# A hybrid encoder layer on one core: inputs laid out by the host, and the input stage written out in order on three engines

## The chip, the cores and the metric

The kernel runs on one core of a Trainium2 chip. The metric is the device time of one launch in microseconds: 2149.15 us is the median of three runs of the kernel before (2146.5 to 2149.57).

Five engines of the core work side by side, each through its own queue of instructions: TensorE (PE in the profile, its weight loads PEld), VectorE (DVE), ScalarE (ACT), GpSimd (POOL) and SyncE (SP), which here issues nearly all transfers. They wait for each other through semaphores. An instruction that waits holds up everything behind it in its engine's queue.

## The reference

The layer has a token-mixing and a channel-mixing half. Only the first steps matter for the change:

```python
mod = (c_act @ w_ada[l] + b_ada[l])[:, None, :]
shift_t, scale_t, gate_t, shift_f, scale_f, gate_f = jnp.split(mod, 6, axis=-1)
h = x * (1.0 + scale_t) + shift_t
proj = h @ w_in[l]
qkv_a, z_a, beta_raw, a_raw, q_b, k_b, v_b, gates = jnp.split(proj, IN_SPLITS, axis=-1)
```

`c_act` is silu of a vector of 1024, `w_ada` is 1024 x 6144, `x` is 1024 tokens x 1024 features, `w_in` 1024 x 9232. From `proj` the layer forms a gated DeltaNet (8 heads, a delta rule in chunks of 64 tokens) and an attention over the own chunk and the 8 before it (16 heads), merges both by sigmoid gates, projects, adds and normalises; then an up projection to 2 x 2816, a causal convolution of width 3, a gated product, a down projection and a second normalisation. All is float32.

## The kernel before, in words

**Data.** `h` is kept with features on the 128 partitions, in 8 chunks of 128 features (`hh`, `hl`: 128 x 8 x 1024). Every float32 operand of a large product is split into a high part (rounded to the format that TensorE takes at full pace) and a low part, the rest; a product is then three: high x high, high x low, low x high. A dense block is 128 output columns: 2 halves of 512 tokens x 8 chunks x 3 products = 48 products of shape 128x512.

**The input stage** (lines 346 to 453) makes `h` and its first uses. For each chunk j of 128 features it

- loads the 1024 x 128 columns of `w_ada` for shift and for scale (`wa`, 1 MB) and 128 columns of `x` (`xj`, 512 KB);
- sums `w_ada` times `csil` = silu(c) over the 8 row blocks on DVE (`acc`, L371 and L373: one scalar product, then seven fused multiply-adds). The first two chunks are summed alone (256 columns an instruction), the other six in pairs (512 columns);
- adds over the partitions with two fp32 products against a column of ones (`pmods`, L407), which TensorE runs as two instructions each;
- adds the bias on ACT (L410), transposes the eight 128 x 128 blocks of `x` on PE (`px`, L416), and applies scale and shift on ACT twice per half of 512 tokens, once in float32 (`h32`, L417) and once rounded (`hh`, L418); DVE takes the difference (`hl`, L419).

While the chunks arrive, three blocks of `w_in` are already multiplied chunk by chunk (`dense_chunk`, `pfirst`, products of L290): the first head's keys and queries and the first gate block, "k", "g" and "q". Chunk j's products are traced two chunks behind its modulation (`LAG0 = 2`). 3 x 48 = 144 products result. After them come 32 products for the beta and decay columns (`pabt`, L447), eight small transposes (`pab`), and the per-feature vectors, each loaded as rows and transposed on PE (`vectors`, `pv`, L323).

**What sets the order.** A planner that simulates the engines and transfers places each instruction in its engine's queue. `tc.issue_after(ins)` puts what is traced in its block behind `ins` on the same engine; in the input stage it is used only to keep the DVE sums one behind the other and a few late loads behind the last `x`. Further on, from the first head on, PE's order is written out by hand (`lane.pinned`): waves of the delta rule between the dense products of the next head.

**Transfers.** All weights are read from the reference's arrays. A block of 128 columns is 1024 runs of 512 bytes (`kview`); `w_up` likewise; the rows of `w_ada` for the gates are 2 KB, those of `w_down` and `w_o` 4 KB. `load_split` loads into a ring of three buffers (`raw`), ACT makes the high part (L188), POOL or DVE the low part (L191).

`class Chain` (L162) wraps an engine: each instruction issued through it stands behind the one before. Before the change it is used only in the later stages.

Of the kernel before, what the change touches and what calls it, by code (L numbers as in the profile page):

```python
# [17 lines left out]
P = 128  # L18
S = 1024
D = 1024  # L20
NK = 8
# [26 lines left out]
HEAD0 = 8  # L48
FILL = (120, 124, 100, 112, 125, 130, 140, 110)
# [12 lines left out]
def _at(group, step_, n, first=0):  # L62
# [8 lines left out]
    "acc0": _at("G", 256, 2, 2048), "acc1": _at("G", 512, 2), "v0": _at("G", 128, 4, 2816), "rab": _at("G", 0, 1, 3328), "abt": _at("G", 0, 1, 1024),  # L71
# [69 lines left out]
def hybrid_layer(  # L141
# [40 lines left out]
    def load_split(h, l, src, he, le, a=1, cuts=1):  # L182

        raw = W.tile([P, 1024], F32, tag="raw", bufs=RB, name=nm("raw"))
        SP.dma_start(raw.rearrange("p (a b) -> p a b", a=a) if a > 1 else raw, src)
        if cuts == 1:
            return split(h, l, raw, he, le)
        he.copy(h, raw)  # L188
        for i in range(cuts):
            N = slice(1024 // cuts * i, 1024 // cuts * (i + 1))  # L190
            le.tensor_tensor(l[:, N], raw[:, N], f(h[:, N]), ALU.subtract)  # L191

    def kview(w, c0, n):
        return w[:, c0:c0 + n].rearrange("(k p) n -> p k n", p=P)

    x2, out2 = x[0], out[0]
    w_ada2, w_in2 = w_ada[0], w_in[0]
# [116 lines left out]
    def vectors(o, group, eng=SP):  # L314

        v = ring("v0", [P, P])
        r = 0
        for s_ in group:
            n = s_.shape[0]
            eng.dma_start(v[r:r + n, :], s_)  # L320
            r += n
        pv = pbank(nm("pv"), "px")
        PE.transpose(pv[:, :r], v[:r, :], ident[:r, :r])  # L323
        ACT.copy(vt[:, o:o + r], pv[:, :r])

    def rows(v):
        return v.rearrange("(r p) -> r p", p=P)
# [4 lines left out]
    GC = 7 * D + 2 * HA  # L332
# [3 lines left out]
    vectors(VO["c"], [c.rearrange("o (r p) -> (o r) p", p=P), rows(b_ada[0])], ACT)  # L336
# [12 lines left out]
    def ab_weights():  # L349
        raw = ring("rab", [P, NK, 16])  # L350
        SP.dma_start(raw, kview(w_in2, 4 * D, 16))
        wab = ring("wab", [P, NK, 32], F32R)
        split(wab[:, :, 0:16], wab[:, :, 16:32], raw, DVE, DVE)
# [4 lines left out]
        ACT.activation(al, al, AF.Exp)  # L358
        return wab, al, dtb

    def ada_cols(j, n):
        kk = NK // 2 // n
        wa = [ring("wa", [P, kk, 2, n * P]) for _ in range(2 * n)]
        for i in range(2 * n):
            for m in range(2):
                SP.dma_start(wa[i][:, :, m, :],
                             w_ada2[kk * P * i:kk * P * i + kk * P, m * D + j * P:m * D + j * P + n * P].rearrange(
                                 "(k p) n -> p k n", p=P))
        acc = ring(f"acc{n - 1}", [P, 2, n * P])
        with tc.issue_after(mark0["acc"]) if mark0 else nullcontext():  # L370
            DVE.tensor_scalar(acc, wa[0][:, 0], csil[:, 0:1], None, ALU.mult)  # L371
            for k in range(1, NK):
                i = DVE.scalar_tensor_tensor(acc, wa[k // kk][:, k % kk], csil[:, k:k + 1], acc,  # L373
                                             ALU.mult, ALU.add)
        mark0["acc"] = i.ins
        for q in range(n):
            accs[j + q] = acc[:, :, q * P:q * P + P]
            xs.append(load_x(j + q))

    def load_x(j):  # L380
        xj = ring("xj", [P, NT, P])
        mark0["x"] = SP.dma_start(xj, x2[:, j * P:j * P + P].rearrange("(t p) n -> p t n", p=P)).ins
        return xj

    LEAD, LAG = 2, LAG0

    first = {"k": (D, "d", "d"), "g": (GC, "m", "m"), "q": (0, "d", "i")}
    wfirst, pend = {}, {}

    def first_weights(m):  # L390
        wfirst[m] = wblock(kview(w_in2, first[m][0], P), NK, ACT, DVE)

    def dense_chunk(k):
        for m in first:
            if m not in pend:
                pend[m] = [pbank(nm("pfirst"), r) for r in first[m][1:]]
            for n in range(2):
                mark0["mm"] = mm_fm(pend[m][n], wfirst[m], hhk, hlk, n, [k]).ins

    xs = []  # L400
    for j in range(LEAD):
        ada_cols(j, 1)
        first_weights("kg"[j])
    for j in range(NK):
        pm = pmods[:, 2 * j:2 * j + 2]
        for m in range(2):
            PE.matmul(pm[:, m:m + 1], accs[j][:, m, :], ones[:, 0:1], start=True, stop=True)  # L407
        cs = ring("mc", [P, 2])
        for m in range(2):
            ACT.activation(cs[:, m:m + 1], pm[:, m:m + 1], AF.Identity, bias=bb[:, j, m:m + 1])  # L410
        h32 = ring("h32", [P, S])
        for n in range(2):
            N = slice(512 * n, 512 * n + 512)
            px = pbank(nm("px"), "px")
            for t in range(4):
                tr = PE.transpose(px[:, t * P:t * P + P], xs[j][:, 4 * n + t, :], ident)  # L416
            ACT.activation(h32[:, N], px, AF.Identity, bias=cs[:, 0:1], scale=cs[:, 1:2])  # L417
            ACT.activation(hh[:, j, N], px, AF.Identity, bias=cs[:, 0:1], scale=cs[:, 1:2])  # L418
# [1480 lines left out]
```

## Time and profile before

The profile shows one execution. Its busy times by engine are shares of the span, the time from the first to the last instruction.

| | us |
|---|---|
| median of three runs | 2149.15 |
| the profiled execution, whole | 2149.37 |
| its span | 2147.7 |
| PE busy | 2101.4 |
| DVE busy | 1428.9 |
| ACT busy | 988.3 |
| POOL busy | 430.8 |
| queue 1, transfers: share of 16 engines | 39.3% |

A line of the profile names a line of the kernel, an engine, an operation and tiles as out<-in, with the shape in partitions x elements. Products are pipelined: one takes about 0.4 us, but the next one starts 0.23 us after it. The view of the stretches gives busy time per engine between two moments; the chain of waits follows what released each instruction, back from the end.

### The profile page before, as it was taken

To read this page: it belongs to the slowest core of one execution; us is meant where nothing else is said; L and a number is where in the kernel's file an instruction comes from. 1 tells how busy PE (TensorE), PEld (TensorE's weight loads), DVE (VectorE), ACT (ScalarE), POOL (GpSimd) and SP (SyncE) were. 2 spreads that over 40 slices of the span, in tenths; PEclk is the share of its full clock that TensorE was granted. 3 is DMA by queue.
4 is the path that set the end of the run, shared out by engine and by line. 5 is a ranking of instruction groups with operands and counts; after the bars stand their busy time and mean duration, and the time that the engine had idled before them with its cause. 6 is when DMAs were issued, how large, how long until landed. Compare 5 with 4: busy or idle time off the path is not lost.

```text
span 2147.7 us, 31798 instructions
## 1 busy us (share of the span) xinstructions
PE 2101.4 (98%) x11577; PEld 1762.4 (82%) x11577; DVE 1428.9 (67%) x3008; ACT 988.3 (46%) x2159; POOL 430.8 (20%) x391
## 2 busy tenths in 40 slices
PE   7999999999999999999999999999999999999998
PEld 5787788888887888989897888888788888888886
DVE  6478576776777754556556534358987788875744
ACT  4544453454544434565555532236554444452431
POOL 0233233233332322110211224200210000000000
PEclk9999999999999999999999999999999999999999
DMA  9232324333233244544547443422332222285440
GB/s 298 68 104 82 123 77 121 99 91 118 72 116 124 63 143 144 158 130 110 161 124 228 140 134 117 142 89 79 98 96 66 85 89 89 98 283 183 162 157 40
DMA packets 243167, 263.04 MB, mean 122 GB/s; under 512 B 23034, under 2 KB 189491, under 8 KB 243011
## 3 DMA queue, kind: packets, MB, share of 16 engines
q1 hardware_dynamic: 242931, 260.99, 39.3%
q8 instruction: 91, 1.49, 0.3%
q14 instruction: 65, 0.53, 0.1%
q10 hardware_dynamic: 80, 0.03, 0.0%
HBM read 207.89 MB, written 58.83 MB: 124 GB/s over the span
## 4 chain that ended last, share of the span: by engine, by line
PE 84%; DVE 8%; ACT 3%; DMA 2%; issue 2%; SPq 1%; POOL 0%; DVEq 0%; ACTq 0%; POOLq 0%
PE pup L1617 17%; PE pdn L1771 11%; PE pqkv L532 7%; PE pqk L532 6%; PE pgt L532 6%; PE pv L532 5%; PE pwo L1459 4%; PE pbr L290 4%; PE pbr L532 4%; PE po L532 4%; PE pz L532 4%; PE ps L532 3%; PE pp L532 2%; PE pfirst L290 1%; DMA raw<-in_w_in_dram 1%
## 5 line engine op out<-in xcount | busy, mean ns | idle before, releaser
L191 POOL TENSOR_TENSOR wl<-raw,wh 128x512 fp32r<-128x512 f32 x170 | 223.7, 1339 | 529.5 <-ACT wh L188 434.4
L1617 PE MATMUL pup<-hh,wop 128*128 128x512 f32 x704 | 224.2, 390 | 0.4 <-ACT G L1654 0.4
L1617 PE MATMUL pup<-t,wop 128*128 128x512 f32 x792 | 189.4, 392 | 1.3 <-DVE cc L1658 0.8
L1617 PEld LDWEIGHTS pup<-t,wop 128*128 128x128 f32 x792 | 148.6, 188 | 34.7 <-DVE cc L1658 1.2
L1771 PE MATMUL pdn<-dop,dop 128*128 128x512 f32 x696 | 161.6, 391 | 0.0
L1617 PEld LDWEIGHTS pup<-hh,wop 128*128 128x128 f32 x704 | 132.1, 188 | 29.1 <-ACT G L1654 0.8
L1771 PEld LDWEIGHTS pdn<-dop,dop 128*128 128x128 f32 x696 | 130.7, 188 | 28.3
L532 PE MATMUL pqkv<-hh,wl 128*128 128x512 f32 x352 | 141.3, 401 | 0.0
L532 PE MATMUL pqkv<-hh,wh 128*128 128x512 f32 x352 | 140.1, 398 | 0.0
L532 PE MATMUL pqkv<-hl,wh 128*128 128x512 f32 x352 | 139.9, 398 | 0.0
L1617 PE MATMUL pup<-hl,wop 128*128 128x512 f32 x352 | 137.2, 390 | 0.0
L188 ACT CAST wh<-raw 128x1024 fp32r<-128x1024 f32 x88 | 92.1, 1046 | 89.1 <-DMA raw<-in_w_branch_b_dram 13.4
L1659 POOL TENSOR_TENSOR cc<-cc,G 128x512 f32<-128x512 f32 x22 | 44.4, 2018 | 375.6 <-DVE G L1641 352.4
L1237 ACT ACTIVATE G<-G,ST 128x640 f32<-128x640 f32 (+4 forms) x128 | 89.3, 698 | 56.4 <-DVE ST L1233 55.8
L177 ACT CAST wop<-wr 128x512 fp32r<-128x512 f32 x104 | 61.7, 620 | 97.9 <-DVE wr L1599 67.0
L532 PE MATMUL pqk<-hh,wh 128*128 128x512 f32 x256 | 105.6, 413 | 0.0
L532 PE MATMUL pqk<-hl,wh 128*128 128x512 f32 x256 | 104.1, 407 | 0.0
L532 PE MATMUL pqk<-hh,wl 128*128 128x512 f32 x256 | 103.4, 404 | 0.0
L532 PE MATMUL pgt<-hh,wh 128*128 128x512 f32 x240 | 99.2, 413 | 0.0
L757 DVE TENSOR_TENSOR FT<-FT,G 128x16 f32<-128x16 f32 (+30 forms) x248 | 92.1, 371 | 8.9 <-POOL G L658 2.5
L532 PE MATMUL pgt<-hh,wl 128*128 128x512 f32 x240 | 96.2, 401 | 0.0
L1264 DVE TENSOR_TENSOR pl<-pp,ph 128x512 fp32r<-128x512 f32 (+1 forms) x112 | 72.9, 651 | 34.8 <-ACT ph L1263 34.1
(409 smaller groups left out, 5482.6 us busy)
## 6 DMA issues: line engine op xcount, KB each, us to landing
raw<-in_w_in_dram SPq DMA_DIRECT2D x72, 512.0 KB
wr<-in_w_up_dram SPq DMA_DIRECT2D x44, 512.0 KB
dwr<-in_w_down_dram SPq DMA_DIRECT2D x44, 512.0 KB
raw<-in_w_ada_dram SPq DMA_DIRECT2D x32, 512.0 KB
qk_d<-SA SPq DMA_DIRECT2D x80, 128.0 KB
wa<-in_w_ada_dram SPq DMA_DIRECT2D x32, 256.0 KB
gates_d<-GT SPq DMA_DIRECT2D x32, 256.0 KB
g_d<-G SPq DMA_DIRECT2D x15, 512.0 KB
```

What stands on the lines that cost most here:

```text
L177: he.copy(h, src)
L188: he.copy(h, raw)
L191: le.tensor_tensor(l[:, N], raw[:, N], f(h[:, N]), ALU.subtract)
L290: i = PE.matmul(ps, a[:, k, :], r[k][:, 512 * n:512 * n + 512], start=(k == 0 and a is wh and r is rh), stop=(k == NK - 1 and a is wl))
L532: r = getattr(PE, op)(*args, **kw)
L757: DVE.tensor_tensor(pr[:, :, 0:i + 1], ft[:, :, 0:i + 1], fa[:, i:i + 1, 0:i + 1].to_broadcast([P, 8, i + 1]), ALU.mult)
L1237: ACT.activation(sb[:, 0:n], sb[:, 0:n], AF.Exp, bias=mx[:, nb - 1:nb], scale=-1.0, accum_out=total_of(hd, t))
L1264: DVE.tensor_tensor(pl[:, B, :], pp, f(ph[:, B, :]), ALU.subtract).ins)
L1459: PE.matmul(ps[n], a[:, t, k, :], wo[k][b][:, 512 * n:512 * n + 512], start=(k == 0 and a is mh and b == 0), stop=(k == NK - 1 and a is ml))
L1617: i = PE.matmul(ps, a[:, u, k, :], b[v][k], start=(new and k == 0 and u == 0 and v == 0), stop=(k == 3 and u == 1), skip_group_check=not new)
L1659: self.later(7, lambda: POOL.tensor_tensor(o, o, self.t, ADD))
L1771: PE.matmul(ps[n], self.g[:, u, i * P:i * P + P], self.w[v][:, 512 * n:512 * n + 512], start=(first and u == 0 and v == 0), stop=(last and ...
```

## The change

The host puts the inputs into another layout, so that a load takes one run per partition: `w_in`, `w_up` and the branch weights as blocks of 128 x 1024 with 4 KB per partition, `w_ada` in the order of the loads, `x` also transposed, and the small vectors already in columns. The transposes of `x` and of the vectors on PE fall away.

The input stage is traced anew. PE, DVE and ACT each get a `Chain`, so the order in these three queues is that of the code below. `DSUM` names the chunks whose modulation is still summed on DVE (2, 3, 5, 6, each alone, 256 columns an instruction); for the others (0, 1, 4, 7) PE forms the sum directly, 8 fp32 products against a column of `csil` for shift and 8 for scale. `EARLY` = 24 fp32 products of the tile of ones stand first in PE's queue; their result is not used.

```diff
+DSUM = (2, 3, 5, 6)
+EARLY = 24
...
-        load_split(wh, wl, src, he, le, a, cuts)
+        load_split(wh, wl, src, he, le, cuts)
...
+    def vectors(o, v, eng=SP):
+        eng.dma_start(vt[:, o:o + v.shape[1]], v)
...
+    pe, dve, act = Chain(PE, None), Chain(DVE, None), Chain(ACT, None)
...
+    def fetch(j):
+        wa = [ring("wa", [P, 4, 2, P]) for _ in range(2)]
+        for i in range(2):
+            SP.dma_start(wa[i].rearrange("p k m n -> p (k m n)"), w_col[2 * j + i])
+        was.append(wa)
+        xj = ring("xj", [P, S])
+        mark0["x"] = SP.dma_start(xj, xt2[j * P:j * P + P, :]).ins
+        xs.append(xj)
...
+    def split_weights(m):
+        raw, wh, wl = wfirst[m]
+        if m != "k":
+            act.copy(wh, raw)
+        for N in (slice(0, 512), slice(512, 1024)):
+            dve.tensor_tensor(wl[:, N], raw[:, N], f(wh[:, N]), ALU.subtract)
+        wfirst[m] = [t_.rearrange("p (k n) -> p k n", k=NK) for t_ in (wh, wl)]
+
+    def dense(m, k):
+        if m not in pend:
+            pend[m] = [pbank(nm("pfirst"), r) for r in first[m][1:]]
+        wh, wl = wfirst[m]
+        for a, r in ((wh, hh), (wl, hh), (wh, hl)):
             for n in range(2):
...
+                pe.matmul(pend[m][n], a[:, k, :], r[:, k, 512 * n:512 * n + 512],
+                          start=(k == 0 and a is wh and r is hh), stop=(k == NK - 1 and r is hl))
+
+    def modulate(j):
         pm = pmods[:, 2 * j:2 * j + 2]
         for m in range(2):
-            PE.matmul(pm[:, m:m + 1], accs[j][:, m, :], ones[:, 0:1], start=True, stop=True)
+            if j in accs:
+                pe.matmul(pm[:, m:m + 1], accs[j][:, m, :], ones[:, 0:1], start=True, stop=True)
+            else:
+                for k in range(NK):
+                    pe.matmul(pm[:, m:m + 1], was[j][k // 4][:, k % 4, m, :], csil[:, k:k + 1],
+                              start=(k == 0), stop=(k == NK - 1))
+
+    def scaled(j):
         cs = ring("mc", [P, 2])
+        pm = pmods[:, 2 * j:2 * j + 2]
         for m in range(2):
-            ACT.activation(cs[:, m:m + 1], pm[:, m:m + 1], AF.Identity, bias=bb[:, j, m:m + 1])
-        h32 = ring("h32", [P, S])
+            act.activation(cs[:, m:m + 1], pm[:, m:m + 1], AF.Identity, bias=bb[:, j, m:m + 1])
+        h32s.append(ring("h32", [P, S]))
+        for q, o in enumerate((hh[:, j], h32s[j])):
+            if q and j == 0:
+                act.copy(wfirst["k"][1], wfirst["k"][0])
+            for n in range(2):
+                N = slice(512 * n, 512 * n + 512)
+                act.activation(o[:, N], xs[j][:, N], AF.Identity, bias=cs[:, 0:1], scale=cs[:, 1:2])
+
+    def lows(j):
         for n in range(2):
             N = slice(512 * n, 512 * n + 512)
...
+            dve.tensor_tensor(hl[:, j, N], h32s[j][:, N], f(hh[:, j, N]), ALU.subtract)
+
+    def summed(j, ks):
+        if 0 in ks:
+            accs[j] = ring("acc0", [P, 2, P])
+            dve.tensor_scalar(accs[j], was[j][0][:, 0], csil[:, 0:1], None, ALU.mult)
+        for k in ks:
+            if k:
+                dve.scalar_tensor_tensor(accs[j], was[j][k // 4][:, k % 4], csil[:, k:k + 1], accs[j],
+                                         ALU.mult, ALU.add)
+
+    h32s = []
+    fetch(0)
+    first_weights("k")
+    fetch(1)
+    first_weights("g")
+    first_weights("q")
+    fetch(2)
+    fetch(3)
+    LO, HI = range(4), range(4, NK)
+    early = pbank("early", "px")
+    for i in range(EARLY):
+        pe.matmul(early[:, 0:P], ones, ones, start=True, stop=True)
+    modulate(0)
+    scaled(0)
+    lows(0)
+    split_weights("k")
+    dense("k", 0)
+    modulate(1)
+    scaled(1)
+    lows(1)
+    dense("k", 1)
+    split_weights("g")
+    dense("g", 0)
+    dense("g", 1)
+    split_weights("q")
+    dense("q", 0)
+    summed(2, LO)
+    summed(2, HI)
+    modulate(2)
+    scaled(2)
+    dense("q", 1)
+    for j in range(2, NK):
+        if j + 2 < NK:
+            fetch(j + 2)
+        if j == NK - 2:
+            ab = ab_weights()
+        if j + 1 in DSUM:
+            summed(j + 1, LO)
+        lows(j)
+        if j + 1 in DSUM:
+            summed(j + 1, HI)
+        dense("k", j)
+        if j + 1 < NK:
+            modulate(j + 1)
+            scaled(j + 1)
+        dense("g", j)
+        dense("q", j)
+    wab, al, dtb = ab()
+    mark0["mm"] = pe.ins
```

The remaining edits only address the new layout: `wpart(c0)` in place of `kview(w_in2, c0, P)`, whole blocks of `w_row` in `mod_rows`, and `prep`, which builds the arrays on the host.

More of the change, by code (lines that the diff above doesn't have):

```diff
@@ L180, in split, with load_split @@
         return le.tensor_tensor(l, src, f(h), ALU.subtract).ins
-    def load_split(h, l, src, he, le, a=1, cuts=1):
+    def load_split(h, l, src, he, le, cuts=1):
         raw = W.tile([P, 1024], F32, tag="raw", bufs=RB, name=nm("raw"))
-        SP.dma_start(raw.rearrange("p (a b) -> p a b", a=a) if a > 1 else raw, src)
+        SP.dma_start(raw, src)
         if cuts == 1:
@@ L331, in hybrid_layer @@
     eg = ring("eg", [P, HA, NT])
-    GC = 7 * D + 2 * HA
+    GC = 7 * D
     one = ring("one", [P, 1])
     ACT.activation(one, ones[:, 0:1], AF.Exp)
-    vectors(VO["c"], [c.rearrange("o (r p) -> (o r) p", p=P), rows(b_ada[0])], ACT)
+    vectors(VO["c"], c, ACT)
+    vectors(VO["b_ada"], b_col, ACT)
     ACT.activation(csil, vt[:, 0:8], AF.Exp, scale=-1.0)
@@ L350, in ab_weights @@
         raw = ring("rab", [P, NK, 16])
-        SP.dma_start(raw, kview(w_in2, 4 * D, 16))
-        wab = ring("wab", [P, NK, 32], F32R)
-        split(wab[:, :, 0:16], wab[:, :, 16:32], raw, DVE, DVE)
+        SP.dma_start(raw, w_ab)
         al = ring("al", [P, HA])
@@ L357, in ab_weights @@
         SP.dma_start(dtb, dt_bias.partition_broadcast(P).rearrange("p o h -> p (o h)"))
[L358 to L378, printed above, removed]
@@ L400, in hybrid_layer, with ready @@
[L400 to L404, printed above, removed]
+        def ready():
+            wab = ring("wab", [P, NK, 32], F32R)
+            dve.tensor_copy(wab[:, :, 0:16], raw)
+            dve.tensor_tensor(wab[:, :, 16:32], raw, f(wab[:, :, 0:16]), ALU.subtract)
+            act.activation(al, al, AF.Exp)
+            return wab, al, dtb
+        return ready
+    pe, dve, act = Chain(PE, None), Chain(DVE, None), Chain(ACT, None)
@@ new lines, in hybrid_layer @@
+    first = {"k": (D, "d", "d"), "g": (GC, "m", "m"), "q": (0, "d", "i")}
+    wfirst, pend, was, xs = {}, {}, [], []
+    def fetch(j):
[6 more added lines that the diff above has]
+        xs.append(xj)
+    def first_weights(m):
+        raw = W.tile([P, 1024], F32, tag="raw", bufs=RB, name=nm("raw"))
+        SP.dma_start(raw, wpart(first[m][0]))
+        wfirst[m] = [raw] + [W.tile([P, 1024], F32R, tag=t, bufs=WB, name=nm(t)) for t in ("wh", "wl")]
@@ L412, in hybrid_layer @@
+    def lows(j):
         for n in range(2):
             N = slice(512 * n, 512 * n + 512)
[L414 to L418, printed above, removed]
-            DVE.tensor_tensor(hl[:, j, N], h32[:, N], f(hh[:, j, N]), ALU.subtract)
@@ L420, in hybrid_layer @@
-        if j % 2 == 0 and j + LEAD < NK:
-            ada_cols(j + LEAD, 2)
-        if j == 0:
-            first_weights("q")
-        if j == NK - 1:
-            with tc.issue_after(mark0["x"]):
-                wab, al, dtb = ab_weights()
-        if j >= LAG:
-            with tc.issue_after(tr.ins) if PTR else nullcontext():
-                dense_chunk(j - LAG)
-    for k in range(NK - LAG, NK):
-        dense_chunk(k)
+            dve.tensor_tensor(hl[:, j, N], h32s[j][:, N], f(hh[:, j, N]), ALU.subtract)
@@ L439, in hybrid_layer @@
-        vectors(VO["conv_f"] + 88, [rows(conv_ffn[0, 2])])
+        vectors(VO["conv_a"], conv_a)
+        vectors(VO["norm"], norm_a)
+        vectors(VO["ln1g"], g1_col)
+        vectors(VO["ln1b"], b1_col)
+        vectors(VO["conv_f"], conv_ffn)
     abt = ring("abt", [P, S])[0:32, :]
@@ L547, in halves @@
     def halves(name, col0, use, ready=None):
-        w = None if ready else wblock(kview(w_in2, col0, P), NK)
+        w = None if ready else wblock(wpart(col0), NK)
         for n in range(2):
```

114 lines of the change are left out of this document (62 added, 52 removed).

## The prediction

> **What bounds the kernel now.** I read the page's busy shares first, then the busy time of each engine by stretches of the first 74 us, because every moved instruction lies there.
>
> ```profile
> span 2147.7 us, 31798 instructions
> ...
> PE 2101.4 (98%) x11577; PEld 1762.4 (82%) x11577; DVE 1428.9 (67%) x3008; ACT 988.3 (46%) x2159; POOL 430.8 (20%) x391
> ```
> ```profile
> 8.70:21.50 12.80, 9.77 (x31) 7.75 (x32) 10.46 (x21) 7.16 (x12) 0.00 (x0) 1.00 1.08 345
> 21.50:28.50 7.00, 5.31 (x26) 3.34 (x24) 4.69 (x7) 2.50 (x4) 0.00 (x0) 1.00 1.08 336
> 28.50:64.50 36.00, 35.48 (x185) 29.01 (x186) 20.90 (x33) 20.67 (x39) 0.95 (x1) 1.00 0.67 203
> 64.50:74.10 9.60, 8.61 (x41) 4.24 (x40) 5.25 (x11) 6.53 (x12) 8.88 (x8) 1.00 0.63 176
> ```
>
> TensorE (PE) is busy 98% of the span, so a microsecond won or lost on its queue in the input stage moves the end by about as much. The stretches hold, in order, the busy time of PE, its weight loads, VectorE (DVE), ScalarE (ACT) and GpSimd, then the granted clock, the DMA share and GB/s. Up to 28.5 us the transfers are saturated (share 1.08) and PE has holes. From 28.5 to 64.5 us PE is full: 35.48 of 36.00. I take 64.5 as the end of the first dense products (pfirst, 144 of them) and 74.1 as the first product of the next projection (pqkv).
>
> The same stretches for the pfirst line alone:
>
> ```profile
> 8.70:21.50 12.80, 5.89 (x11) 3.71 (x12) 1.00 1.08 345
> 21.50:28.50 7.00, 4.13 (x14) 1.95 (x12) 1.00 1.08 336
> 28.50:64.50 36.00, 31.81 (x120) 21.27 (x120) 1.00 0.67 203
> ```
>
> Some 24 of the 144 are done by 28.5 us, the other 120 afterwards without a hole. So the change must either have done more by 28.5 us, or be no less dense after it.
>
> **Prices.** From the timeline (start, duration, engine, line; a last x4 is four instructions drawn together):
>
> ```profile
> 0.90 0.17 DVE L219 MEMSET ones<- 128x128 f32 x1 [0.90 <-PEq L1885]
> ...
> 5.89 0.35 DVE L371 TENSOR_SCALAR G<-wa,csil 128x256 f32<-128x256 f32 x1
> 6.28 3.61 DVE L373 SCALAR_TENSOR_TENSOR G<-wa,csil,G 128x256 f32<-128x256 f32 x7
> ...
> 9.94 1.02 PE L407 MATMUL pmods<-ones,G 128*128 128x1 f32 x4
> ...
> 10.52 1.05 ACT L188 CAST wh<-raw 128x1024 fp32r<-128x1024 f32 x1 [5.31 <-DMA raw<-in_w_in_dram]
> ...
> 11.47 0.41 ACT L410 ACTIVATE G<-pmods,G 128x1 f32<-128x1 f32 x2
> ...
> 11.91 0.78 ACT L417 ACTIVATE h<-px,G 128x512 f32<-128x512 f32 x1
> ...
> 12.59 0.77 ACT L418 ACTIVATE hh<-px,G 128x512 fp32r<-128x512 f32 x1
> ...
> 14.63 0.69 DVE L419 TENSOR_TENSOR hl<-h,hh 128x512 fp32r<-128x512 f32 x1
> ...
> 17.10 0.78 PE L290 MATMUL pfirst<-hh,wh 128*128 128x512 f32 x1
> ...
> 18.54 1.29 DVE L191 TENSOR_TENSOR wl<-raw,wh 128x512 fp32r<-128x512 f32 x2
> ...
> 19.81 0.33 PEld L290 LDWEIGHTS pfirst<-hh,wh 128*128 128x128 f32 x1
> ...
> 30.48 0.40 PE L290 MATMUL pfirst<-hh,wh 128*128 128x512 f32 x1
> ...
> 30.72 0.40 PE L290 MATMUL pfirst<-hl,wh 128*128 128x512 f32 x1
> ...
> 30.72 0.19 PEld L290 LDWEIGHTS pfirst<-hh,wl 128*128 128x128 f32 x1
> ...
> 50.96 0.64 PEld L407 LDWEIGHTS pmods<-ones,G 128*128 128x128 f32 x4
> ...
> 1463.91 1.52 ACT L1448 ACTIVATE r<-r,ST 128x512 f32<-128x512 f32 x2
> ```
>
> From the chain of waits (start, time on the chain):
>
> ```profile
> 51.35 0.34 PE pmods L407 x4
> ...
> 57.14 0.44 PE px L416 x4
> ...
> 116.41 1.78 PE pkk L532 x16
> ```
>
> A dense product costs 0.23 us of PE's queue (30.48 to 30.72), so a chunk's 18 cost 4.1. A pass of ACT over 512 columns costs 0.70 (0.68 between the starts 11.91 and 12.59; 1.52 for two that read SBUF, as the new ones do), a low half on DVE 0.65 to 0.69, a step of the modulation sum 0.52 (3.61/7), the two little ACT operations 0.44 until the next one starts.
>
> **The change part by part.**
>
> *Removed from PE:* 64 transposes of x (0.11 each by the px row: 7.0 us) and four transposes of small vectors. *Added:* for four of the eight chunks the modulation sum goes to PE as 16 fp32 products against one column, two instructions each as in the pmods rows, so 32 a chunk. A long stream of these is not in the trace. Its price lies between 0.085 (0.34/4, products that pipeline behind each other) and 0.16 (0.64/4, their weight loads end to end); I take 0.11, from the nearest long stream of fp32 instructions with a 128x128 load before each (pkk, 1.78/16). That is 3.6 us a chunk (2.7 to 5.1), 14.3 for four, against about 0.4 a chunk before. So PE gains 7 us and pays about 13.
>
> *Warm-up products:* 24 fp32 products are 48 instructions from 1.1 us on (ones is set by 1.07). PE runs at half speed at first: a weight load takes 0.33 at 19.81 and 0.19 at 30.72, and the change of pace falls at 21.5 us (the clock column shows 1.00 throughout, so the durations tell it). Before that change the products had followed each other from 17.1 on, so 4.4 us. At 0.22 cold (pmods at 9.94, less its first) and 0.11 warm, with the clock rising 4.4 us after 1.1, 20 instructions run cold and 28 warm, to 8.6; with a rise two or three microseconds later to 10; with none to 11.7. I take 8.5. The first chunk's products are queued behind them, though its columns are there by then: DVE read them from 6.28 on.
>
> The Trainium skill, "TensorE: Matmul & The Clock Gate", Part 1, says the clock starts halved and is released after about 3.4 us of sustained activity. The before trace does not contradict this: its products came with holes until 17 us. By that rule the products end near 8.5, which is my value; without it, near 11.7, which would add 3 us to the sum.
>
> *The order pinned on three queues.* This is the large term. On PE the sum of chunk j+1 stands behind dense("k", j), whose last two products need the low halves of chunk j; on DVE the second half of the sum of chunk j+1 stands behind these low halves; on ACT the four passes of a chunk run hh first, then h32. So from one chunk's modulation to the next runs one chain through PE, ACT and DVE, and behind the waiting modulation on PE stand the products of g and q, which nobody else can start. The start, from 8.5: modulation 0 to 12.1; ACT's small pair, two hh passes, the copy of k's weights (1.05) and two h32 passes to 16.6; low halves to 17.3; the first half of wl to 18.0; four products to 18.9. Modulation 1 to 22.5, ACT to 26.0, low halves to 26.7, then on DVE the splits of g and q (1.29 each) to 29.4 and the whole sum of chunk 2 (0.35 + 7 x 0.52) to 33.5. By 28.5 us 18 dense products have run, against 24 before. Then, from modulation to modulation:
>
> - both summed on DVE (2 to 3, 5 to 6): 0.6 + 0.4 + 2.9 (ACT) + 0.7 (low) + 2.1 (four sum steps) + 0.1 for hand-overs = 6.8
> - DVE, then PE (3 to 4, 6 to 7): 0.6 + 0.4 + 2.9 + 0.7 + 0.4 = 5.0
> - PE, then DVE (4 to 5): 6.8 + 3.2 = 10.0
> - the last: 3.8 + 0.4 + 2.9 + 0.7 + 0.4, then 12 products of g and q, 2.7 = 10.9
>
> Sum: 33.6 + 6.8 + 5.0 + 10.0 + 6.8 + 5.0 + 10.9 = 78.1, against 64.5. PE's own work in these chunks is 4.5 or 7.7 each; the difference is hole.
>
> *After it.* Of the 9.6 us to pqkv, three vector transposes and the wait for their copy go:
>
> ```profile
> 69.80 0.26 PE L323 MATMUL pv<-ident,G 44*128 44x44 f32 x1
> ...
> 70.34 0.41 PE L447 MATMUL pabt<-hh,wab 128*32 128x512 f32 x1 [0.29 <-ACT vt L324]
> ```
>
> 3 x 0.27 + 0.3, about 1.2, leaves 8.4: 86.5 against 74.1, so +12.4 us.
>
> *Contiguous weights.* The transfers from 10 to 50 us, then those of the down projection, whose rows are 2 and 4 KB already (queue: packets, MB, share of 16 engines):
>
> ```profile
> DMA packets 21358, 13.40 MB, mean 335 GB/s; under 512 B 1481, under 2 KB 21356, under 8 KB 21356
> ...
> q1 hardware_dynamic: 21356, 13.38, 107.1%
> ```
> ```profile
> q1 hardware_dynamic: 15433, 44.62, 58.9%
> ```
>
> Engine time per MB is 51 us in the first (16 x 40 x 1.071 / 13.38) and 46 in the second (16 x 220 x 0.589 / 44.62): a tenth better, so a chunk's 1.57 MB comes in 4.3 us instead of 4.7. On SyncE's queue the loads of chunks 0 to 3 and the three first weights go out at once and are down by 25 us; those of chunk 6 wait for the sum of chunk 2 (33.5), those of chunk 7 for chunk 3's (40), with the small vectors and the next weights behind them, and land some 7 us later, at 41 and 47, while they are needed at 55 and 67. The loads are hidden; without that cover the faster ones would gain 0.4 us a chunk. GpSimd's queue has one fill that waits for pmods and then the splits of the next weights, which wait for the end of k's products in both kernels; it moves with the stage.
>
> Later in the kernel PE waits, after 74 us, for (first, second and last of nine listed; us, times, longest):
>
> ```profile
> PE pp L532 <- DVE pl L1264: 9.0, 6, 3.7
> PE py L532 <- ACT G L796: 2.6, 1, 2.6
> ...
> PE pvn L532 <- ACT po L590: 0.7, 1, 0.7
> ```
> ```profile
> 1156.88 5.62 DMA raw<-oa_d
> ...
> 1166.45 0.85 PE pbr L532 x2
> ...
> 1171.69 1.16 PE pbr L532 x5
> ```
>
> None names a weight load; the longest, 3.7, hangs on a read of oa_d that keeps its layout. Shorter loads beside it, and a remainder that is planned anew, are worth between -5 (that wait and the slow products after it) and +2; I take -2.
>
> **Sum.** The profiled execution took 2149.4 (span 2147.7 and 1.7 around it), 0.2 over the median of the runs. 2149.4 + 12.4 - 2.0 = 2159.8, so 2160. Bounds: the one-column stream at 0.085 or 0.16 lies on the path in all four chunks, -3.2 or +6.4; warm-up -0.5 or +3.2; remainder -3 or +4. Not all fall on one side at once; the likeliest case spans 2153 to 2169.
>
> **Rivals.**
>
> *The clock falls again after the warm-up (15%), 2165.* PE idles from 12.1 to 15.1 and again to 18.0. For it: behind the 3.7 us wait at 1162 two products take 0.85, twice the 0.23 that five show later (1.16). Against it: 3.0 is less than 3.7. Modulation 1 would then cost 7.0 instead of 3.6, the rest of the first chunks 1.6 more: +5. The Trainium skill, same page, "Why this matters for your kernels", wants no idle gap above about 3 us, so these holes are at its edge; the trace's one case, 3.7 us, agrees.
>
> *Chunks are bound by PE alone (17%), 2143, faster.* If ACT's and DVE's part of the loop were hidden, the queue would need 33.1 for 144 products and 16.1 for modulations from 8.5 on, plus the first chunk's hole of 5.4: 63.1, and 8.4 to pqkv makes 71.5, -2.6; with -2 for the remainder 2144.8, and 2141.6 with the stream at 0.085: the middle. It decides once the mean from modulation to modulation is under 5.9 us. For it: DVE is relieved of half its sums, and ACT and DVE are busy only 21 of 36 us in the dense stretch. Against it: the order in the code puts these steps behind one another.
>
> *The remainder pays the stage back (10%), 2151.* PE's nine listed waits after 74 us sum to about 20; were the new plan to remove half, 2149.4 + 12.4 - 10.5. Against it: they hang on softmax and solve steps that stay.
>
> **How the numbers follow.** Forecast 58%, clock 15%, PE alone 17%, remainder 10%. No change is what lies within 0.2% (2145 to 2153.5): most of the last case, little of the others, 8%; faster 17%; slower 75%. The range of 8 in 10 cuts most of the faster case and little above: 2146 to 2169.
>
> **What would show it.** Right: pfirst ends near 78 us, PE holes of 1 to 3 us ahead of modulations 2, 3, 5 and 6 whose releaser is DVE's sum, and no wait on a transfer after 10 us. Each step: the 48 first products end at 8 to 10 us with the 0.19 loads behind them; 32 one-column products in 3.6 us. Wrong: pfirst over by 65 us, or modulations under 6 us apart with PE full; then the loop is not the bound. A remainder that differs by more than 5 us would break the -2.

## The result, and the profile after

The changed kernel took 2172.9 us (median; 2170.9 to 2177.7), the kernel before beside it 2148.8: a ratio of 1.0116, 95% interval 1.0103 to 1.0129. Slower, as forecast, but by 24 us instead of 11, and outside the range. One execution each of three kernels below, of 3496 to 11767 us, belongs to a slow state and is left out of the medians.

The page of the changed kernel: span, busy shares, granted clock by slices.

```profile
span 2171.3 us, 31920 instructions
...
PE 2129.5 (98%) x11668; PEld 1787.2 (82%) x11668; DVE 1424.7 (66%) x3000; ACT 992.6 (46%) x2156; POOL 430.7 (20%) x391
...
PEclk7899999999999999999999999999999999999999
```

PE is busy for 28 us more, though the work added is about half of that: 7.4 of warm-up products as they ran and 14.3 of one-column products at the forecast's price, less 7.0 of transposes. The clock row begins with a 7 and an 8 (a slice is 54 us), so most of the lost time lies in the first 108 us. The same stretches as before the change (busy time of PE, its loads, DVE, ACT, POOL, then granted clock, DMA share, GB/s):

```profile
8.70:21.50 12.80, 8.28 (x45) 7.09 (x45) 2.59 (x4) 4.29 (x7) 0.00 (x0) 0.62 1.03 421
21.50:28.50 7.00, 5.65 (x25) 5.26 (x25) 0.00 (x0) 1.86 (x5) 0.00 (x0) 0.50 0.65 246
28.50:64.50 36.00, 33.31 (x128) 25.50 (x128) 20.73 (x41) 15.87 (x28) 0.00 (x0) 0.76 0.51 177
64.50:74.10 9.60, 7.96 (x29) 5.94 (x28) 4.62 (x8) 4.22 (x8) 0.96 (x1) 0.82 0.00 0
```

Before, the clock column shows 1.00 in all of these, but the record of the clock begins with its first rise, there at 21.5 us. Up to then PE ran at half speed before the change too, as the weight loads in the prediction tell (0.33 us at 19.81, 0.19 at 30.72); from 21.5 on the clock stayed full through the stage. Now it is up from 4.9 us on, but only 0.50 to 0.82 in these stretches, and in the long one PE is busy 33.3 of 36.0 us but runs 128 instructions instead of 185. The transfers are the better part of it: 421 GB/s instead of 345, and no product waits for one after 10 us.

The timeline of PE, only the warm-up products, the modulations, and the first products behind the stage (start, duration, line, tiles, shape, idle time ahead):

```profile
1.12 7.43 PE L172 MATMUL early<-ones 128*128 128x128 f32 x48 [1.12 <-DVE ones L228]
...
8.38 3.75 PE L172 MATMUL pmods<-csil,wa 128*128 128x1 f32 x32
...
19.75 6.82 PE L172 MATMUL pmods<-csil,wa 128*128 128x1 f32 x32
...
37.41 0.61 PE L172 MATMUL pmods<-ones,G 128*128 128x1 f32 x4 [1.34 <-DVE G L172]
...
44.16 0.61 PE L172 MATMUL pmods<-ones,G 128*128 128x1 f32 x4 [1.35 <-DVE G L172]
...
50.45 4.75 PE L172 MATMUL pmods<-csil,wa 128*128 128x1 f32 x32
...
61.34 0.61 PE L172 MATMUL pmods<-ones,G 128*128 128x1 f32 x4
...
68.11 0.61 PE L172 MATMUL pmods<-ones,G 128*128 128x1 f32 x4 [1.45 <-DVE G L172]
...
74.40 4.80 PE L172 MATMUL pmods<-csil,wa 128*128 128x1 f32 x32
...
88.01 0.39 PE L502 MATMUL pabt<-hh,wab 128*32 128x512 f32 x1
...
95.41 0.40 PE L587 MATMUL pqkv<-hh,wh 128*128 128x512 f32 x1
```

The eight rows of pmods are modulations 0 to 7. The stage ends at 88.0 (forecast 78.1) and pqkv starts at 95.4 (forecast 86.5; 74.1 before): +21.3 us. From there to the end the kernel takes 2075.9 us, before 2073.6: +2.3. The profiled execution before took 2149.4; 2149.4 + 21.3 + 2.3 = 2173.0, what the profiled execution now took.

What the clock does shows when the same view is cut at its own steps, which lie 3.41 us apart:

```profile
8.34:11.76 3.42, 3.42 (x33) 3.42 (x33) 0.00 (x0) 0.00 (x0) 0.00 (x0) 1.00 1.03 420
11.76:15.17 3.41, 0.42 (x4) 0.34 (x3) 0.00 (x0) 2.97 (x6) 0.00 (x0) 0.50 1.02 419
...
35.65:39.07 3.42, 2.08 (x11) 1.49 (x10) 3.21 (x8) 0.99 (x3) 0.00 (x0) 1.00 0.95 364
39.07:42.48 3.41, 3.41 (x8) 1.68 (x7) 1.82 (x4) 2.36 (x4) 0.00 (x0) 0.50 0.87 273
...
49.30:52.72 3.42, 3.42 (x28) 3.19 (x26) 1.37 (x3) 0.00 (x0) 0.00 (x0) 1.00 0.00 0
52.72:56.13 3.41, 3.41 (x16) 3.22 (x16) 0.00 (x0) 0.86 (x3) 0.00 (x0) 0.50 0.02 5
```

And the pfirst products alone in two of these windows:

```profile
35.65:39.07 3.42, 1.61 (x7) 1.05 (x6) 0.00 (x0) 0.00 (x0) 1.00 0.95 364
...
49.30:52.72 3.42, 1.31 (x6) 0.74 (x4) 0.00 (x0) 0.00 (x0) 1.00 0.00 0
```

The clock was full up to 11.76. From 8.34 to 11.76 PE is busy without a break, with the one-column products of modulation 0, and the next window runs at half the clock. From 35.65 it idles 1.3 us and has 1.61 us of dense products; the next window is at half. From 49.30 it is busy throughout, 1.31 us of it dense, the rest one-column products: again half. So one-column products look like idleness to the clock, and no hole of 3 us is needed. Between 11.8 and 83.4 us, 13 windows are at half the clock, 44.4 us (the expectation of c_fill below speaks of ten).

### The profile page after: what moved, and what is told of

It is laid out like the page before. It is cut to its first block, busy times and chain, and to the rows that moved or that the text cites. A ratio compares the mean times of both kernels' runs of the same rounds, so it can differ in the third digit from the quotient of the medians.

```text
span 2171.3 us, 31920 instructions
## 1 busy us (share of the span) xinstructions
PE 2129.5 (98%) x11668; PEld 1787.2 (82%) x11668; DVE 1424.7 (66%) x3000; ACT 992.6 (46%) x2156; POOL 430.7 (20%) x391
## 4 chain that ended last, share of the span: by engine, by line
PE 80%; DVE 7%; ACT 3%; DMA 2%; issue 1%; SPq 0%; POOL 0%; DVEq 0%; ACTq 0%; POOLq 0%
PE pup L1669 17%; PE pdn L1823 11%; PE pqkv L587 8%; PE pqk L587 7%; PE pgt L587 5%; PE pv L587 5%; PE pwo L1511 4%; PE pbr L299 4%; PE po L587 4%; PE pbr L587 3%; PE pz L587 3%; PE ps L587 2%; PE pp L587 2%; DVE FT L812 1%; DVE FT L814 1%
## 5 line engine op out<-in xcount | busy, mean ns | idle before, releaser
L190 ACT CAST wh<-raw 128x1024 fp32r<-128x1024 f32 x85 | 88.8, 1047 | 81.6 <-PE pqkv L587 12.4
L1711 POOL TENSOR_TENSOR cc<-cc,G 128x512 f32<-128x512 f32 x22 | 44.4, 2018 | 375.0 <-DVE G L1693 352.0
```

Of the source, the lines that this page charges most:

```text
L1711: self.later(7, lambda: POOL.tensor_tensor(o, o, self.t, ADD))
```

## The experiments

The theory: the pinned chain costs about the forecast's 12 us, and the half clock, which the one-column products and the holes of that chain bring, the other 9 in the stage. The rival: layout, transfers or a worse plan of the later stages. The table gives the median, the ratio to the kernel before on the same chip with its 95% interval, the start of pqkv in the profile, the rest of the span behind that start, and how many windows of 3.41 us in that rest, without its last 10 us, ran at half the clock. The kernel before took 2147.5 to 2148.8 in the four sets of runs. The profile is of one execution, which need not be the median: it took 2166.1 for a_noearly, 2150.8 for l_start, 2148.7 for f2_pool and 2140.9 for i_fill.

| kernel | us | ratio | interval | pqkv starts | rest | half windows |
|---|---|---|---|---|---|---|
| before | 2148.8 | 1 | | 74.1 | 2073.6 | 1 |
| changed | 2172.9 | 1.0116 | 1.0103 to 1.0129 | 95.4 | 2075.9 | 3 |
| e_layout | 2144.6 | 0.9982 | 0.9973 to 0.9991 | 68.7 | 2073.3 | 1 |
| b_dve | 2161.6 | 1.0060 | 1.0048 to 1.0073 | 87.2 | 2073.0 | 2 |
| d_ahead | 2164.7 | 1.0074 | 1.0060 to 1.0088 | 90.6 | 2074.6 | 2 |
| h_both | 2155.3 | 1.0036 | 1.0023 to 1.0048 | 81.1 | 2072.0 | 2 |
| l_start | 2147.8 | 1.0003 | 0.9994 to 1.0012 | 72.8 | 2076.2 | 4 |
| c_fill | 2167.4 | 1.0087 | 1.0073 to 1.0101 | 94.2 | 2072.7 | 2 |
| g_spread | 2173.2 | 1.0111 | 1.0095 to 1.0127 | 95.8 | 2074.9 | 3 |
| a_noearly | 2169.6 | 1.0110 | 1.0095 to 1.0126 | 92.4 | 2072.0 | 2 |
| f_layout_early | 2141.2 | 0.9969 | 0.9958 to 0.9981 | 68.2 | 2070.8 | 2 |
| i_fill | 2143.5 | 0.9977 | 0.9967 to 0.9988 | 65.9 | 2073.3 | 3 |
| f2_pool | 2144.6 | 0.9987 | 0.9979 to 0.9996 | 69.8 | 2077.1 | 4 |
| j_pool_fill | 2148.4 | 1.0000 | 0.9991 to 1.0009 | 75.2 | 2074.5 | 3 |

The last two columns go together. With the new layout and two half windows the rest takes 2072.5 us on average (2070.8 to 2074.6), with three 2074.6 (2073.3 to 2075.9), with four 2076.2 and 2077.1. A window at half the clock can cost up to 1.7 us. So a good part of the scatter of the rest is the clock again; what brings these windows was not tried.

### The layout alone (e_layout)

The new input stage is replaced by one in the manner of the kernel before; the layout stays. In the diffs from here on, "..." stands for lines that are not shown, and the words behind # are explanations.

```diff
-    pe, dve, act = Chain(PE, None), Chain(DVE, None), Chain(ACT, None)
-    ... (fetch to the last dense("q", j): the order written out)
+    for j in range(LEAD):
+        fetch(j)                 # loads and the whole sum of chunk j on DVE
+        first_weights("kg"[j])
+    for j in range(NK):
+        ...                      # pmods, cs, then per half h32, hh, hl
+        if j + LEAD < NK:
+            fetch(j + LEAD)
+        if j >= LAG:
+            dense_chunk(j - LAG)
```

> The host layout alone: the planner orders the stage as in the kernel before, all sums on VectorE (one chunk at a time), x is read transposed, no first products, nothing pinned. Theory (the loss is made inside the stage, by the pinned order and by the half clock that its one-column streams and holes bring): with 64 transposes off a full TensorE (7.0 us) and faster loads, pfirst ends near 57 to 60 and the time is 2140 to 2144, 29 to 33 below the changed kernel. Rival (layout or the new plan of the later stages carries part of the loss): 2150 or above, and the later stages are 2 us or more longer than in the kernel before.

Measured 2144.6, 4 below the kernel before and 28 below the changed one. So the loss is made inside the stage, as the theory says; this run takes away the pinned order, the one-column products and the warm-up together and does not tell them apart. The time is 0.6 above the theory's range, and pfirst ends at 61.5 instead of 57 to 60. The rest of the span is as long as before (2073.3 against 2073.6), so the rival falls. Its own first chunks show why the stage gained only 5.4 us:

```profile
13.00:21.00 8.00, 5.89 (x17) 4.13 (x18) 7.39 (x15) 4.49 (x9) 0.00 (x0) 1.00 1.03 421
21.00:28.00 7.00, 7.00 (x19) 5.36 (x20) 6.89 (x15) 5.38 (x9) 0.00 (x0) 0.51 1.03 420
```

DVE is full (7.39 of 8.00, 6.89 of 7.00), and PE runs 19 instructions in 7 us at a clock of 0.51. The 1.00 of the first row again hides a late first rise, at 17.7 us.

### Sums of chunks 4 and 7 on DVE (b_dve)

```diff
-DSUM = (2, 3, 5, 6)
+DSUM = (2, 3, 4, 5, 6, 7)
```

> The changed kernel with the sums of chunks 4 and 7 on VectorE too (2 to 7 there, 0 and 1 on TensorE). By the steps of the forecast the loops come out the same, five of 6.8 instead of 6.8 + 5.0 + 10.0 + 6.8 + 5.0: +0.4. Theory (one-column streams do not count as activity, so they bring the half clock): the half clock behind modulations 4 and 7 goes and the time falls by 4 to 8, to about 2167. Rival (the chain alone): 2173, within 2 us of the changed kernel.

Measured 2161.6, 11.3 less: more than the theory gave, and far from the rival's 2173. The rival was priced too high, though. By the forecast's own steps the last loop, behind modulation 7, falls from 10.9 to 7.7 (measured 7.9), which the +0.4 leaves out, so the chain alone would give about 2170. In the profiles the stage is 8.2 us shorter: some 2.8 of it are this sum, and the other 5.4 go with the half windows, 9 instead of 13. The rest of the span is 3.0 shorter, with one half window fewer. The modulations in its timeline:

```profile
37.69 0.61 PE L172 MATMUL pmods<-ones,G 128*128 128x1 f32 x4 [1.12 <-DVE G L172]
...
44.45 1.01 PE L172 MATMUL pmods<-ones,G 128*128 128x1 f32 x4 [1.46 <-DVE G L172]
...
51.77 0.50 PE L172 MATMUL pmods<-ones,G 128*128 128x1 f32 x4
...
58.43 0.61 PE L172 MATMUL pmods<-ones,G 128*128 128x1 f32 x4 [1.46 <-DVE G L172]
...
65.19 0.61 PE L172 MATMUL pmods<-ones,G 128*128 128x1 f32 x4 [0.34 <-DVE G L172]
...
71.95 0.61 PE L172 MATMUL pmods<-ones,G 128*128 128x1 f32 x4 [1.46 <-DVE G L172]
```

They lie 6.76, 7.32, 6.66, 6.76 and 6.76 apart, and the forecast's loop for two sums on DVE was 6.8. The one longer loop holds two half windows (43.3 to 50.1); a third one (60.4 to 63.8) only ate the hole ahead of the modulation at 65.19. The chain was sized rightly; the clock was what it lacked.

### The next chunk ahead (d_ahead), and both edits (h_both)

```diff
         if j + 1 in DSUM:
-            summed(j + 1, LO)
-        lows(j)
-        if j + 1 in DSUM:
-            summed(j + 1, HI)
-        dense("k", j)
+            summed(j + 1, range(NK))
         if j + 1 < NK:
             modulate(j + 1)
             scaled(j + 1)
+        lows(j)
+        dense("k", j)
         dense("g", j)
```

> The changed kernel with one order undone: from chunk 2 on the whole sum of chunk j+1, its modulation and its four passes stand ahead of the low halves and the products of chunk j. Amount of work the same. Theory (the chain PE, ACT, DVE, PE of the pinned order is worth the forecast's 12 us): modulations come 4.5 to 7.7 us apart instead of 5 to 11, the stage ends 11 to 17 earlier, time 2156 to 2162. Rival (the chain is not what paces; VectorE's sum and low halves, 5.4 a chunk, or the half clock of the streams do): at most 6 us, 2167 or above.

Measured 2164.7: 8.3 less, between the two. The chain paces, but undoing it does not give back all it should: the stage ends 4.8 us earlier, not 11 to 17. Its timeline shows what holds the rest:

```profile
48.17 4.56 PE L172 MATMUL pmods<-csil,wa 128*128 128x1 f32 x32
...
59.08 0.50 PE L172 MATMUL pmods<-ones,G 128*128 128x1 f32 x4
...
63.66 0.50 PE L172 MATMUL pmods<-ones,G 128*128 128x1 f32 x4
```

After 59.1 a chunk takes 4.6 us, what 18 products and a modulation need at full clock. The one with the one-column products takes 10.9 instead of 7.7, with no hole in it: PE at half clock. h_both is this order with all sums from chunk 2 on DVE.

> Two edits at once in the changed kernel: sums of chunks 2 to 7 on VectorE, and from chunk 2 on the next chunk's sum, modulation and passes ahead of the low halves and products of this one. Alone they took off 11.3 and 8.3 us. Theory (a chain and, on top of it, the half clock): VectorE now paces with 4.0 for a sum and 1.4 for low halves, modulations lie 5.4 apart from 37.7 on, pfirst ends near 73, the next projection starts near 80.5, time 2157 (2154 to 2160): what is then left of the loss lies ahead of 37.7. Rival 1 (both edits only take away the same half windows): 2161, as the second alone. Rival 2 (they act apart from each other): the sum of both, 2153.

Measured 2155.3, as the theory had it (2154 to 2160); pqkv starts at 81.1 against 80.5. From 49.7 on the modulations lie 5.1 apart; the loop ahead of that takes 8.3 and holds two half windows (39.0 to 45.8). Rival 1 (2161) misses. Rival 2 (2153) is not excluded: the interval of the ratio stands for 2152.7 to 2158.1. Modulation 2 still starts at 37.41, so what is left of the loss lies ahead of it.

### And chunk 1's sum on DVE (l_start)

```diff
-DSUM = (2, 3, 4, 5, 6, 7)
+DSUM = (1, 2, 3, 4, 5, 6, 7)
...
     scaled(0)
+    summed(1, range(NK))
     lows(0)
```

> As the kernel with both edits (2155.3), and in addition chunk 1's sum on VectorE, ahead of the low halves of chunk 0, so that only modulation 0 is a block of one-column products. Theory (what is left of the loss lies ahead of 37.7: the second block of one-column products, 6.8 us at half the clock, in the chain): modulation 1 ends near 20.5 instead of 26.6 and modulation 2 starts near 31.5 instead of 37.4; time 2148 to 2150, as the kernel before. Rival (ScalarE's passes, VectorE's splits or the transfers pace the first chunks): at most 2 us, 2153 or above.

Measured 2147.8, ratio 1.0003: the kernel before. That is 0.2 below the theory's range, and the rival (2153 or above) falls. In its timeline modulation 1 is a sum of four short instructions, and modulation 2 comes 5.2 us sooner:

```profile
20.57 0.85 PE L172 MATMUL pmods<-ones,G 128*128 128x1 f32 x4
...
32.25 0.61 PE L172 MATMUL pmods<-ones,G 128*128 128x1 f32 x4 [1.26 <-DVE G L172]
```

So three edits of order and place, with the layout, the three chains and the warm-up products kept, take the whole loss away: 11.3 + 6.3 + 7.5 us by the medians, in the order b_dve, h_both, l_start. Each takes away holes or one-column blocks of the chain and half windows together (13, 9, 8 and 5 in the stage). Against the layout alone (e_layout) some 3 us of loss are left.

### Work added to the holes (c_fill)

```diff
+    def idle(n):
+        for i in range(n):
+            pe.matmul(early[:, 0:P], ones, ones, start=True, stop=True)
     modulate(0)
+    idle(6)
     ...
+    idle(5)
     modulate(2)     # and the same ahead of modulations 3 and 6
```

> The changed kernel with 21 more fp32 products of ones in TensorE's holes: 6 behind modulation 0 and 5 ahead of modulations 2, 3 and 6. Work is added and nothing taken away. Theory (a window of 3.4 us without enough wide products is followed by one at half the clock): the half clock that follows these holes goes, at least three of the ten half windows between 11.8 and 83.4, and the time falls by 3 to 9 us, to about 2167. Rival (the holes are the loss, the clock beside them is not on the path): no gain, 0 to +4, 2173 to 2177.

Measured 2167.4: 21 products more, 5.5 us less. But in the profiled execution only 1.2 us of it are in the stage (pqkv 94.2); the rest of the span is 3.2 shorter, with one half window fewer, which accounts for up to 1.7. The half windows behind modulations 2, 3 and 6 did go, as expected, and the loops 3 to 4 and 6 to 7 both fell from 6.29 to 5.15, near the 5.0 that the forecast gave at full clock. Modulation 2, which starts 0.8 later, and the loop 4 to 5, which takes 0.3 more, take half of these 2.3 us back. The early stretch did not improve:

```profile
8.70:21.50 12.80, 11.05 (x54) 9.65 (x54) 2.59 (x4) 4.29 (x7) 0.00 (x0) 0.59 1.02 418
21.50:28.50 7.00, 5.65 (x25) 5.28 (x25) 0.00 (x0) 1.85 (x5) 0.00 (x0) 0.50 0.84 251
```

The first six products fell into a window that was already at half, and some 2.3 us of them did not lift it. The time came as expected, but by luck in part: the two shorter loops are the clock's, the rest of the 5.5 us is not shown to be.

### The one-column products spread out (g_spread)

```diff
+    def columns(j):              # the 16 products of chunk j, one at a time
+        pm = early[:, 2 * j:2 * j + 2]
+        ...
+                yield
-    def dense(m, k):
+    def dense(m, k, between=iter(())):
 ...
+                if r is hh:
+                    next(between, None)
```

> The changed kernel with the one-column products of chunks 4 and 7 formed one by one between the dense products of the chunks before (into another bank), instead of in one block. The work on each engine is the same. Theory (blocks of one-column products bring the half clock, and they stand in the chain): the half windows behind modulations 4 and 7 go and the chain loses 3.2 us twice, 2160 to 2164. Rival 1 (the chain alone, the clock stays as it is): 2166 to 2168. Rival 2 (TensorE pays for these products wherever they stand): no gain, 2171 or above.

Measured 2173.2: no gain, the number of rival 2. The windows show a reason that the rival did not name, half the clock: first all of PE, then pfirst alone.

```profile
48.32:51.73 3.41, 3.41 (x12) 2.93 (x11) 2.32 (x5) 0.00 (x0) 0.00 (x0) 0.50 0.03 8
51.73:55.15 3.42, 3.42 (x12) 2.93 (x11) 0.00 (x0) 0.00 (x0) 0.00 (x0) 0.50 0.02 5
```
```profile
48.32:51.73 3.41, 3.17 (x6) 1.33 (x4) 0.00 (x0) 0.00 (x0) 0.50 0.03 8
51.73:55.15 3.42, 3.18 (x6) 1.54 (x5) 0.00 (x0) 0.00 (x0) 0.50 0.02 5
```

PE is full, and half of its instructions are one-column products (6 of 12 are dense; their durations overlap the next instruction's). That mixture does not bring the clock back: it stays at half from 44.9 to 58.6 and from 72.2 to 82.5. My theory that a block in one piece is the trouble falls; the count in the last section points to the share of wide products in a window.

### Without the warm-up products (a_noearly)

```diff
-EARLY = 24
+EARLY = 0
```

> The changed kernel without the 24 warm-up products. Theory (the clock falls at 11.8 whatever they do, since modulation 0 is one-column products): only modulation 0 gets slower, 7.0 instead of 3.7 from 6.1 on, so it ends near 13.2 instead of 12.1: +1 us, 2173 to 2175. Rival (the warm-up products carry the first chunks): +4 or more, 2177. Rival 2 (they delay modulation 0 more than they save): faster by 1 or more.

Ratio 1.0110 against 1.0116: no difference that can be told, though the median, 2169.6, misses the theory's 2173 to 2175 and lies on the side of rival 2. No gain of the warm-up shows in this kernel: the window behind it holds one-column products, and the clock falls. Modulation 0 ended at 13.0 instead of 12.1, as expected. By the chance of where the windows fell, the profiled execution kept the full clock from 49.5 to 76.8, and so shows the loops of the changed order without the half clock:

```profile
51.33 3.63 PE L172 MATMUL pmods<-csil,wa 128*128 128x1 f32 x32
...
61.12 0.61 PE L172 MATMUL pmods<-ones,G 128*128 128x1 f32 x4 [1.45 <-DVE G L172]
...
67.88 0.61 PE L172 MATMUL pmods<-ones,G 128*128 128x1 f32 x4 [1.46 <-DVE G L172]
...
73.03 3.63 PE L172 MATMUL pmods<-csil,wa 128*128 128x1 f32 x32
```

4 to 5: 9.79 (forecast 10.0; 10.89 in the changed kernel). 5 to 6: 6.76 (6.8). 6 to 7: 5.15 (5.0; 6.29 in the changed kernel). The 32 one-column products: 3.63 (3.6). So the same chain takes the forecast's time where the clock is full.

### Versions of the layout kernel (f_layout_early, i_fill, f2_pool, j_pool_fill)

To e_layout, f_layout_early adds the 24 warm-up products. i_fill takes 33 of them and puts 9 more behind modulations 0 and 1. f2_pool is f_layout_early with the low parts of the first weights on GpSimd, j_pool_fill is both.

```diff
+    for i in range(EARLY):
+        PE.matmul(early[:, 0:P], ones, ones, start=True, stop=True)
...
-        wfirst[m] = wblock(wpart(first[m][0]), NK, ACT, DVE)
+        wfirst[m] = wblock(wpart(first[m][0]), NK, ACT, POOL)
```

> The layout with the planner's order of the stage, and the 24 warm-up products ahead of it. Without them this kernel took 2144.6 and its first dense products ran at half the clock until 17.7. Theory (a window without enough wide products is followed by half the clock): the products end near 8.5, TensorE then idles until the first dense product near 13, and the clock is down again by then: within 1.5 us of 2144.6. Rival (the clock, once up, lasts): the products from 13 to 17.7 take half as long and the time is 2140 to 2142.

Measured 2141.2, in the rival's range; but not for the rival's reason: the clock was down again from 11.1 to 17.9, as the theory said, and pqkv starts only 0.5 us sooner. The intervals of the two ratios overlap, so the difference from e_layout is not settled. It has the lowest median, and it is faster than both kernels.

> The layout with the planner's order and the warm-up products (2141.2), with 33 of them instead of 24 and 9 more behind each of the modulations 0 and 1, where TensorE had holes of 2.0 us. Theory (at full clock a window of 3.4 us with under some 45% of wide products is followed by one at half; at half clock it takes one with over 80% to bring it back): the clock stays up from 4.3 on, the dense products between 13 and 28 take half as long, 2 to 4 us less, 2137 to 2139. Rival (VectorE's sums pace this stretch, so faster products only wait): 2140 to 2143.

The stretches of i_fill:

```profile
8.70:21.50 12.80, 11.96 (x78) 9.76 (x77) 12.15 (x26) 8.94 (x15) 0.00 (x0) 1.00 1.03 419
21.50:28.50 7.00, 6.91 (x32) 5.11 (x31) 6.82 (x16) 3.90 (x7) 0.00 (x0) 1.00 1.02 419
28.50:64.50 36.00, 31.92 (x148) 23.82 (x147) 27.09 (x56) 24.49 (x41) 7.25 (x7) 1.00 0.47 175
```

The clock is 1.00 in all three, and from 4.7 us on through the whole stage, which no other kernel here has; pqkv starts at 65.9, 2.3 us sooner. So the clock did what the theory said; yet the time (2143.5) misses both ranges and is not below f_layout_early. DVE is full to 28.5 (12.15 of 12.80, 6.82 of 7.00), which is the rival's reason. The 2.3 us are lost again in the rest of the span (2073.3 against 2070.8), which holds three half windows instead of two.

> The layout with the planner's order and the warm-up products (2141.2), with the low parts of the three first weights made on GpSimd instead of VectorE (six operations of 0.65 us there). Theory (VectorE is full from 5.9 to 33 and its sum of chunk 1 is late): 2 to 4 us less, 2137 to 2139. Rival (GpSimd takes near 1.1 us for each, so the first weight's low part comes later than now and holds the first products): 2141 to 2143.

> Both: low parts of the first weights on GpSimd, and warm-up products in the first holes. Theory (VectorE and the half clock each hold the first chunks): the gains add up, 2134 to 2137. Rival: no better than the better of the two alone.

Measured 2144.6 and 2148.4: both theories wrong; the first is 1.6 above its rival's range, the second as its rival said. Rows of GpSimd, DVE and PE in f2_pool:

```profile
9.86 2.53 POOL L193 TENSOR_TENSOR wl<-raw,wh 128x512 fp32r<-128x512 f32 x2 [4.50 <-ACT wh L190]
```
```profile
9.99 1.28 DVE L378 TENSOR_SCALAR G<-wa,csil 128x256 f32<-128x256 f32 x1
...
15.16 1.76 DVE L411 TENSOR_TENSOR hl<-h,hh 128x512 fp32r<-128x512 f32 x1
```
```profile
14.38 0.79 PE L299 MATMUL pfirst<-hl,wh 128*128 128x512 f32 x1 [0.88 <-DVE hl L411]
```

GpSimd takes 1.3 to 1.7 us for each half against 0.65 on DVE, so the first weight's low part is there at 12.4 instead of 11.4. But no product waits for it. While GpSimd works at two low parts (9.86 to 12.39, 15.08 to 18.05), DVE's own instructions take longer: 1.28 us instead of 0.35 for the first step of a sum, 1.76 instead of 0.69 for a low half. PE then waits 0.88 and 0.95 us for low halves of chunk 0, which it does not do in f_layout_early. So DVE is slower beside GpSimd here; that this costs the whole difference is not shown.

## Why the prediction was wrong, point by point

**The bound: right.** A microsecond on PE's queue in this stage moved the end by about as much: over these kernels pqkv starts between 65.9 and 95.8, while the rest of the span keeps within 2070.8 and 2077.1.

**Warm-up: right in itself.** The 48 instructions were through at 8.4 (8 to 10 forecast). That they would carry the next chunks was taken for granted, and wrong.

**One-column products: price right, place of the price wrong.** 3.75 and 3.63 at full clock (3.6 forecast). But the price was used four times, and they cost 3.75, 6.82, 4.75 and 4.80: 20.1 instead of 14.3.

**The chain: right, at full clock.** From modulation 2 the forecast's loops were 6.8, 5.0, 10.0, 6.8, 5.0 and 10.9. The changed kernel has 6.75, 6.29, 10.89, 6.77, 6.29 and 13.6: the two loops between sums that fall on DVE agree (a half window in the first of them only ate its hole), and the other four, each of which holds half windows, are longer; all six together by 6.1. The start is 3.8 late: modulation 1 took 3.2 more, and it began 0.9 late. By 28.5 us some seven dense products had run, not 18. Behind the stage the 7.4 us to pqkv are 1.0 less than forecast. 3.8 + 6.1 - 1.0 = 8.9, the difference between 95.4 and 86.5. Of the holes that were to show it, those ahead of modulations 2, 3 and 6 are there (1.34, 1.35 and 1.45 us, released by DVE's sum); the one ahead of 5 is not, for PE at half the clock filled it.

**The step that failed** is the rival of the clock. It was seen, given 15%, and sized at "+5", for "Modulation 1" and "the rest of the first chunks". What spoke "against it" was that "3.0 is less than 3.7", the longest hole of the trace taken as the condition. In fact the clock fell at 11.8, before the hole of 3.0 us had begun (12.1). The runs put another condition in the place of the hole's length: the share of wide products in a window of 3.41 us. By it the forecast's own loops, with a hole of 1.3 us each, and its own streams of one-column products could bring the half clock again and again, and did so up to 83 us. The rival's price for modulation 1 was right (7.0; measured 6.82); its extent was not. All prices of the sum, 0.11 and 0.23, were full-clock prices; the stage came out 8.9 us longer than the forecast, of the 13.2 us by which the profiled execution missed.

**Transfers: right.** They got faster by the trace and were hidden.

**The remainder: -2 is not borne out.** It was +2.3 in the profile, the other 4.3 of the 13.2 us; over all kernels with the layout it scatters from -2.8 to +3.5 around the 2073.6 of before. The changed kernel has three half windows there and the kernel before one, up to 3.4 us by estimate (2 x 1.7), so most of this miss may be the clock too. That contiguous weights gain something in the later stages is not shown, nor that they lose.

**The other rivals.** PE alone, deciding under 5.9 us from modulation to modulation: 7.4 on average. The remainder did not pay anything back.

## What to carry to other kernels

Price PE's work by two clocks: cut the stage into windows of 3.4 us and count how much of each is wide products; products against one column are holes for this count, however dense they stand. A chain that leaves a third of PE idle costs its holes and can cost the half clock that they bring, so break it by order (the next chunk's small steps ahead of this chunk's products) before filling it. Warm-up products kept the clock up only where wide products followed at once (i_fill), and even there no gain in time is settled.

## What the runs showed of the hardware

**When the clock falls and rises.** I laid the product records of all fourteen profiles over the windows of 3.413 us up to 92 us, and took for each the share of time in which a product against at least 128 columns ran, each counted to the start of the next product at most. After a window at full clock: with a share up to 0.44, half followed in 30 of 30; between 0.45 and 0.52 in 5 of 14; from 0.53 on in 1 of 211. After a window at half clock (the time ahead of the first rise among them): with a share up to 0.75, full followed in 0 of 71; from 0.83 on in 50 of 52. Both fit one measure: work of about 0.4 to 0.5 of what a full-clock window holds (0.83 at half clock is 0.41). The bounds are read from these same profiles; i_fill alone was forecast with such bounds, and its clock came as forecast.

The Trainium skill, "TensorE: Matmul & The Clock Gate", Part 1, describes a free-running window of 3413 ns; the steps of the clock here lie at multiples of 3.41 us, and their phase differs from run to run, which agrees. The Trainium skill, same page, "Why this matters for your kernels", names a gap above about 3 us as the limit; here holes of 1.35 us were enough, and full windows of one-column products without any gap, so the measurement decides against it.

**Luck of the phase.** The windows are not tied to the program: in the kernels with 24 warm-up products the first rise comes at 3.9 to 6.9 us. So whether a stream fills one or is cut by two can change the time. The changed kernel's runs lie within 7 us, a_noearly's within 9, and the mean granted clock of a_noearly's runs goes with their time: 0.995, 0.993, 0.993 and 0.992 for 2166.1, 2169.6, 2169.7 and 2175.2 us. That the phase is what differs between these runs is not shown, for each kernel has one profile.
